# One core of a two-layer hybrid decoder trunk: side work in more steps, new wait numbers, a branch hint

## The chip, the core and the metric

The kernel runs on one core of a Trainium2 chip. A core has five engines, each with an instruction queue of its own that is worked off in order: TensorE (PE: matmuls, with weight loads shown apart as PEld), VectorE (DVE), ScalarE (ACT), GpSimd (POOL) and SyncE (SP), which here only issues DMA transfers. An engine waits for another through semaphores, and an instruction that waits holds all that stand behind it on its queue. The metric is the device time of one execution in microseconds (us).

## The reference

Two layers over 256 tokens of width 1024, all in float32:

```python
for i in range(2):
    h = rmsnorm(x, norm_mix[i])
    z, xbc, dt, nsa_q, nsa_kv, nsa_g, rwkv_u, swa_q, swa_kv, gates = split_cols(h @ w_in[i])
    y = [ssd(z, xbc, dt), nsa(nsa_q, nsa_kv, nsa_g), rwkv7(rwkv_u), swa(swa_q, swa_kv, positions)]
    merged = sum(sigmoid(gates[m]) * (y[m] @ w_br[m]) for m in range(4))
    x = x + merged @ w_out[i]
    h = rmsnorm(x, norm_ffn[i])
    x = x + (swiglu(h) if i % 2 == 0 else moe_top2_of_8(h))
    x = x + sigmoid(x @ ple_gate[i]) * (p[i] @ ple_proj[i])
return rmsnorm(x, norm_final)
```

The four mixers are a chunked state-space scan (ssd), sparse attention (nsa), a recurrent state update (rwkv7) and sliding-window attention (swa). Only swa uses `positions`: its queries and keys are rotated by `cos` and `sin` of position times 32 inverse frequencies.

## The kernel before

**The main stream.** The program is one list of units, worked through by `run_units` (L195). A unit is a weight panel: SP loads it as `raw` (128 x 1024 float32 at most, four buffers, L269); ACT casts it to a rounded half `H` (`L318`); DVE (`L321`) and POOL (`L323`) together make the residual `L = raw - H`, DVE three quarters of the columns and POOL one. `H` and `L` have three buffers. PE then multiplies with three products, `H` times high, `L` times high, `H` times low (`mm3`, L362 to L364). Units named `tokm` give tokens by 416 or 512 columns, units named `fm` give features by 256 tokens. The activations' own halves are made in the same way by `split_to`: a cast on ACT (`L371`) and a subtraction on DVE (`L372`). In a trace a tile's name tells what it is: `qTH` and `qTL` the halves of a query, `krH` and `krL` those of the rotated key, `yeH` that of an expert's output.

**The side work.** The mixers' own work, all that is not a product with a weight panel, is written as Python generators in a list `side`: `rwkv_half` (twice a layer), `ssd`, `nsa`, `swa`, and in layer 0 also `rope_tables` (the rotary tables, L516 to L542) and `cast` (constants to bf16, L172). The main stream calls `tick()` at fixed points between its matmuls. A tick takes 0.64 off every generator's counter, and a generator whose counter is used up emits its next step, up to its next `yield`. How many ticks it then rests stands in the table `WAITS`, by the generator's name with the count of its use and by the number of the step; where the table has no entry, the yielded number divided by 0.64 and rounded up holds (1.2 where nothing is yielded). So the table sets where in each engine's queue a step's instructions stand between the instructions of the main stream; nothing is moved at run time. All of it is in one in-order queue per engine: a side step that waits on POOL or ACT holds the next panel's `L` or `H` there.

**The names in the steps.** In `rwkv_half`: `v`, `k`, `r` are shifted mixes (L672 on ACT, L673 on DVE), `kkn` (L770), `kp` (L774 DVE, L775 POOL), `AR` (L780 DVE, L781 POOL), `beta` (L783, L785), `bq` (L792), then the matmuls `bop` (L797) and `gram` (L823); `kap` (L787) is POOL's. `LO` and `XT` (L838, L846) belong to the inversion of a triangular matrix, with the matmuls `m`, `dx`, `dxt` (L812). In attention, `nm` (L1141, DVE) is a row maximum and `Pm` (L1145, ACT) the exponential that follows it; `rraw` (L1368) is a query or key copied out for the rotation, which takes a matmul (L1385), two operations on DVE (L1387, L1389: `rtmp`) and one on POOL (L1388), and then `split_to`. In `ssd`, `wT` is a decay (L1071 on ACT, L1072 on DVE).

**The end.** Layer 1 ends with eight experts. `overflow` (L1994 to L1998) is a branch on a value read on the chip: where an expert has more than 128 tokens, a second pass of all experts runs; with these inputs it doesn't, and each engine jumps over that pass. What follows is the sum of the last expert's output (`yeH`, `sct`) and the last per-layer product.

Of the kernel before, what the change touches and what calls it, by code (L numbers as in the profile page):

```python
# [19 lines left out]
P = 128  # L20
# [28 lines left out]
def _consts():  # L49
# [37 lines left out]
    for k, v in cols.items():  # L87
# [10 lines left out]


WAITS = {  # L100
# [19 lines left out]
}  # L120


def trunk_kernel(tc, I, out, dbg=None, upto=99):
# [38 lines left out]
    def late_consts(place):  # L162
        stages = []
        for c in range(NC32, NCST, 512):
            w = min(512, NCST - c)
            stages.append((c - NC32, w, place("stage")))
            nc.sync.dma_start(stages[-1][2][:, :w], I["consts"][:, c:c + w])

        def cast():
            yield 8.0  # L170
            for c, w, t in stages:
                nc.gpsimd.tensor_copy(cstb[:, c:c + w], t[:, :w])  # L172
        return cast

    def K(name):
        o, w = COFF[name]
        return cst[:, o:o + w] if o < NC32 else cstb[:, o - NC32:o - NC32 + w]
# [16 lines left out]
    def psb(name="psb"):  # L194
        return psB.tile([P, 512], F32, tag="b", name=name)  # L195
# [24 lines left out]
    def wait_of(g, d):  # L220
        return WAITS.get(g[2], {}).get(g[3], math.ceil(d / 0.64 - 1e-3)) * 0.64

# [25 lines left out]
    def until(*names):  # L248
        while not all(n in flags for n in names):
            yield "poll"  # L250
# [118 lines left out]
    def split_to(H, L, src, scale=None):  # L369
        if scale is None:  # L370
            nc.scalar.copy(H, src)  # L371
            tt(L, src, H, ALU.subtract)  # L372
        else:
            act(H, src, AF.Copy, scale=scale)  # L374
            stt(L, src, scale, H, ALU.mult, ALU.subtract)  # L375
# [19 lines left out]
    def dma2(dst, src):  # L395
        nc.sync.dma_start(dst, src)
# [121 lines left out]
    def rope_tables(place):  # L518

        pool = nc.gpsimd  # L520
        pos, scr = place("pos"), place("scr")
        posi = pos.bitcast(I32)[:, 0:S]
        ang, nn = scr[:, 0:S], scr[:, S:2 * S]
        dma2(posi, I["positions"].to_broadcast([P, S]))
        pool.tensor_copy(ang, posi)
        pool.tensor_scalar(ang, ang, K("invf"), None, ALU.mult)
        magic = 12582912.0
        pool.tensor_scalar(nn, ang, 1.0 / (2 * math.pi), magic, ALU.mult, ALU.add)
        pool.tensor_scalar(nn, nn, magic, None, ALU.subtract)
        c1 = 6.28125  # L530
        c2 = 0.0019350051879882812
        c3 = 2 * math.pi - c1 - c2
        for c in (c1, c2, c3):
            pool.tensor_scalar(cosT, nn, -c, None, ALU.mult)
            pool.tensor_tensor(ang, ang, cosT, ALU.add)
        yield 12.0
        ts(ang, ang, math.pi, -math.pi, ALU.min, ALU.max)
        stt(nn, ang, -1.0, ang, ALU.mult, ALU.max)
        ts(nn, nn, -1.0, math.pi / 2, ALU.mult, ALU.add)
        yield 2.0  # L540
        act(sinT, ang, AF.Sin)
        act(cosT, nn, AF.Sin)  # L542
# [9 lines left out]
    def mixing(l, after):  # L552
        Z = SimpleNamespace(y={}, mxa=None)
# [98 lines left out]
        def branch_out(name, pool, bufs=2):  # L652
            H = pool.tile([P, 4, S], F32R, tag="yH", name="yH" + name, bufs=bufs)
            L = pool.tile([P, 4, S], F32R, tag="yL", name="yL" + name, bufs=bufs)
            Z.y[name] = (H, L)
# [529 lines left out]
        def key_tile(tag, bufs=1):  # L1185

            kz = tuple(Z.mxa.tile([P, 2, S], F32R, tag=tag + c, name=tag + c, bufs=bufs) for c in "HL")
            for t in kz:
                for g in range(2):
                    nc.gpsimd.memset(t[HD[1 - g], g].bitcast(F32), 0.0)  # L1190
            return kz

        def query_tile():
            return tuple(Z.mxa.tile([P, 4, S], F32R, tag="qT" + c, name="qT" + c, bufs=2) for c in "HL")

        def pv(o, voff, PT, first, last):
            for g in range(2):
                sl = HD[g]
                v0 = Z.vtok[:, 0, voff + g * 64:voff + g * 64 + 64]
                v1 = Z.vtok[:, 1, voff + g * 64:voff + g * 64 + 64]  # L1200
                mm(o[sl, 0:S], v0, PT[:, g, 0:S], start=first, stop=False)
                mm(o[sl, P:S], v1, PT[:, g, S:384], start=False, stop=last)
# [173 lines left out]
        def swa():  # L1376
            mxa = Z.mxa
            qs = query_tile()
            ks = key_tile("kr")
            for n in range(5):  # L1380
                yield from until(F(f"rr{n}."))
                yield 2.0
                raw = rr[n]
                rp = psb("rotp")[:, :S]
                mm(rp, K("rot"), raw, start=True, stop=True)  # L1385
                t = mxa.tile([P, S], F32, tag="rt", name="rtmp", bufs=2)
                tt(t, rp, sinT, ALU.mult)  # L1387
                nc.gpsimd.tensor_tensor(raw, raw, cosT, ALU.mult)  # L1388
                tt(t, t, raw, ALU.add)  # L1389
                if n:  # L1390
                    split_to(qs[0][:, n - 1], qs[1][:, n - 1], t)
                else:
                    for g in range(2):
                        split_to(ks[0][HD[g], g], ks[1][HD[g], g], t[HD[g]])
            nsk = mxa.tile([P, 4, 2], F32, tag="nsk", name="nsk")
            ts(nsk, Z.snk.rearrange("p (g r) -> p r g", g=2), -1.0, None, ALU.mult)
            branch_out("swa", Z.mxa, 1)
            def use(PT, r):
                o = psb("so")[:, :S]
                pv(o, 256, PT, True, True)  # L1400
                head_out("swa", r, o)

            yield from until(F("nsa"))
            yield from attn_pipe([(qs, ks, r, None, True, nsk[:, r], lambda PT, r=r: use(PT, r)) for r in range(4)])
            flags.add(F("swa"))
# [40 lines left out]
        if l == 0:  # L1446
            unit(None, spawn=[lambda: rope_tables(R)])
# [287 lines left out]
    def moe(l, Z):  # L1735
# [252 lines left out]

        def load_most():
            Z.most = nc.values_load(Z.mxi[0:1, 0:1], min_val=0, max_val=S)  # L1990
            tc.mark_branch_hint_location("overflow")

        experts(0)

        def overflow():
            with tc.If(Z.most > P, label="overflow"):
                keep = list(stream)
                stream.clear()  # L1998
                experts(P)
                mine = list(stream)  # L2000
                stream[:] = keep
                with tc.tile_pool(name="ovr", bufs=2) as r2, tc.tile_pool(name="ovs", bufs=2) as s2:
                    run_units(mine, Slots(r2, 2, s2, 2))
            if f"xffn{l}" in dbg:
                for i in range(2):
                    nc.sync.dma_start(dbg[f"xffn{l}"][i], x[:, i])
# [5 lines left out]
    for l in range(DEPTH):  # L2012
        if upto <= 10 * l:
            break
        Z = SimpleNamespace(ctx=ExitStack(), GT={}, OHT={}, rc={}, before=None, after=None)
# [35 lines left out]
```

## Time and profile before

| | before |
|---|---|
| median of 3 runs | 2006.41 us (2005.33 to 2008.68) |
| the profiled execution | 2005.13 us |
| its span in the trace | 2003.3 us |
| PE busy | 1938.6 us (97%) |
| DVE, ACT, POOL busy | 77%, 59%, 56% |
| mean granted clock of TensorE | 0.989 |

The span falls into mixing of layer 0 (0 to 475 us), its dense feed-forward block with the per-layer product (475 to 700), mixing of layer 1 (700 to 1160), the experts (1160 to 1950) and the end (1950 to 2003). A timeline row is one or several like instructions in a row: start, busy time, engine, line, operation, output and inputs; in square brackets the idle time of the engine just ahead of it and what ended it. [...]

### The profile page before, as it was taken

What the parts mean: (1) busy time and instruction counts of PE and PEld (TensorE: products, weight loads), DVE (VectorE), ACT (ScalarE), POOL (GpSimd) and SP (SyncE); (2) the same over time, 40 slices, a digit from 0 to 9 for tenths busy, and PEclk for the clock granted to TensorE, in tenths of its full rate; (3) what the DMA queues carried; (4) which work ended last, traced back from release to release, by engine and by line L of the source; (5) the groups of instructions that cost most, each with busy time, mean ns of one, the idle gap of its engine ahead of it and who ended that gap; (6) DMA issues with size and microseconds to landing.
All of it is one profiled execution on the core that took longest, in us unless ns stands there. A gap on an engine that the chain in (4) does not pass through costs nothing. (4 is left out here: it accounts for less than half of the span.)

```text
span 2003.3 us, 37459 instructions
## 1 busy us (share of the span) xinstructions
PE 1938.6 (97%) x13236; PEld 1606.8 (80%) x13236; DVE 1533.7 (77%) x2432; ACT 1176.9 (59%) x1786; POOL 1120.4 (56%) x976
## 2 busy tenths in 40 slices
PE   7999999999999899999999999999999999999997
PEld 6798897778999788878777777778777877787775
DVE  6475756766555666656666589999999999999996
ACT  5333445545444443334455567777877787778773
POOL 4543254454555254414354666777767767777773
PEclk9999999999999999999999999999999999999998
DMA  7322464457665453228354889999999999999973
GB/s 202 96 75 82 111 146 137 117 160 216 187 189 166 115 133 93 76 85 163 102 146 137 280 270 354 313 330 351 360 354 331 347 362 357 328 349 362 354 255 107
DMA packets 419441, 435.78 MB, mean 218 GB/s; under 512 B 67876, under 2 KB 355624, under 8 KB 419240
## 3 DMA queue, kind: packets, MB, share of 16 engines
q1 hardware_dynamic: 419240, 433.26, 69.1%
q8 instruction: 106, 1.74, 0.4%
q14 instruction: 95, 0.78, 0.1%
HBM read 432.13 MB, written 1.05 MB: 216 GB/s over the span
## 5 line engine op out<-in xcount | busy, mean ns | idle before, releaser
L323 POOL TENSOR_TENSOR L<-raw,H 128x256 fp32r<-128x256 f32 (+1 forms) x794 | 950.8, 1207 | 808.7 <-ACT H L318 608.8
L321 DVE TENSOR_TENSOR L<-raw,H 128x768 fp32r<-128x768 f32 (+1 forms) x792 | 933.3, 1207 | 169.2 <-ACT H L318 166.7
L318 ACT CAST H<-raw 128x1024 fp32r<-128x1024 f32 x794 | 828.6, 1047 | 227.0 <-issue 44.8
L362 PE MATMUL gu<-H,GH 128*128 128x512 f32 x704 | 286.5, 407 | 0.1
L363 PE MATMUL gu<-L,GH 128*128 128x512 f32 x704 | 279.3, 397 | 0.5 <-DVE L L321 0.5
L364 PE MATMUL gu<-H,GL 128*128 128x512 f32 x704 | 278.1, 395 | 1.1 <-DVE GL L375 1.1
L364 PE MATMUL dn<-H,aL 128*128 128x512 f32 x440 | 173.9, 395 | 1.6 <-DVE aL L372 1.6
L363 PE MATMUL dn<-L,aH 128*128 128x512 f32 x440 | 174.5, 397 | 0.0
L362 PE MATMUL dn<-H,aH 128*128 128x512 f32 x440 | 174.3, 396 | 0.2 <-ACT pj L1576 0.2
L362 PE MATMUL fm<-hTH,H 128*128 128x256 f32 x560 | 166.9, 298 | 0.0
L363 PEld LDWEIGHTS gu<-L,GH 128*128 128x128 f32 x704 | 132.5, 188 | 41.1 <-DVE L L321 15.0
L363 PE MATMUL fm<-hTL,H 128*128 128x256 f32 x560 | 157.8, 282 | 0.0
L364 PE MATMUL fm<-hTH,L 128*128 128x256 f32 x560 | 157.5, 281 | 0.0
L364 PEld LDWEIGHTS gu<-H,GL 128*128 128x128 f32 x704 | 132.4, 188 | 29.0 <-DVE GL L375 2.7
L362 PEld LDWEIGHTS gu<-H,GH 128*128 128x128 f32 x704 | 132.3, 188 | 27.3 <-ACT GH L374 0.6
L362 PE MATMUL tokm<-H,hTH 128*128 128x512 f32 (+1 forms) x320 | 139.1, 435 | 4.4 <-ACT H L318 4.4
L363 PE MATMUL tokm<-L,hTH 128*128 128x512 f32 (+1 forms) x320 | 126.8, 396 | 5.6 <-POOL L L323 4.0
L364 PE MATMUL tokm<-H,hTL 128*128 128x512 f32 (+1 forms) x320 | 126.4, 395 | 0.0
L362 PEld LDWEIGHTS fm<-hTH,H 128*128 128x128 f32 x560 | 106.4, 190 | 5.9 <-issue 2.7
L363 PEld LDWEIGHTS fm<-hTL,H 128*128 128x128 f32 x560 | 106.4, 190 | 0.2
L364 PEld LDWEIGHTS fm<-hTH,L 128*128 128x128 f32 x560 | 106.2, 190 | 0.0
L363 PEld LDWEIGHTS dn<-L,aH 128*128 128x128 f32 x440 | 82.6, 188 | 23.8 <-DVE L L321 7.6
(507 smaller groups left out, 3520.2 us busy)
## 6 DMA issues: line engine op xcount, KB each, us to landing
raw<-moe_w_gate SPq DMA_DIRECT2D x341, 256.0 KB
raw<-moe_w_up SPq DMA_DIRECT2D x341, 256.0 KB
raw<-moe_w_down SPq DMA_DIRECT2D x169, 512.0 KB
raw<-w_in SPq DMA_DIRECT2D x126, 512.0 KB
raw<-ffn_w_gate SPq DMA_DIRECT2D x22, 512.0 KB
raw<-ffn_w_up SPq DMA_DIRECT2D x22, 512.0 KB
raw<-ffn_w_down SPq DMA_DIRECT2D x22, 512.0 KB
raw<-w_in SPq DMA_DIRECT2D x32, 256.0 KB
```

The source lines that it names most:

```text
L318: nc.scalar.copy(H[:, :n], raw[:, :n])
L321: tt(L[:, :m], raw[:, :m], H[:, :m], ALU.subtract)
L323: nc.gpsimd.tensor_tensor(L[:, m:n], raw[:, m:n], H[:, m:n], ALU.subtract)
L362: mm(o, l[0], r[0], start=start, stop=False)
L363: mm(o, l[0], r[1], start=False, stop=False)
L364: mm(o, l[1], r[0], start=False, stop=stop)
```

## The change

The whole table `WAITS` is written anew. Two generators that had no entries get some, `cast0` and `rope_tables0`, and `swa` has five steps more, so that its entries are counted differently. In the code four places change: `cast` ends a step after each of its three casts; `rope_tables` ends a step after the positions' transfer is issued, after each two of its operations on POOL and after each pair of the last six (before, all ten stood in one step); `swa` ends a step ahead of each rotary split; and the branch gets a hint instruction for all engines that it is likely taken, and is written the other way round (`Z.most <= P` with an empty body and the experts in `Else`, marked as not preferred to fall through). No operation on data is added or removed.

```diff
 WAITS = {
+    'cast0': {0: 18, 1: 1, 2: 5, 3: 6, 4: 1},
...
+    'rope_tables0': {0: 2, 2: 1, 3: 8, 4: 8, 5: 9, 6: 1, 7: 9},
...
             for c, w, t in stages:
                 nc.gpsimd.tensor_copy(cstb[:, c:c + w], t[:, :w])
+                yield
...
         dma2(posi, I["positions"].to_broadcast([P, S]))
+        yield 2.5
         pool.tensor_copy(ang, posi)
         pool.tensor_scalar(ang, ang, K("invf"), None, ALU.mult)
+        yield 1.2
         magic = 12582912.0
         pool.tensor_scalar(nn, ang, 1.0 / (2 * math.pi), magic, ALU.mult, ALU.add)
         pool.tensor_scalar(nn, nn, magic, None, ALU.subtract)
+        yield 1.2
...
         for c in (c1, c2, c3):
             pool.tensor_scalar(cosT, nn, -c, None, ALU.mult)
             pool.tensor_tensor(ang, ang, cosT, ALU.add)
-        yield 12.0
+            yield 1.2
...
                 tt(t, t, raw, ALU.add)
+                yield 1.2
                 if n:
                     split_to(qs[0][:, n - 1], qs[1][:, n - 1], t)
...
             Z.most = nc.values_load(Z.mxi[0:1, 0:1], min_val=0, max_val=S)
-            tc.mark_branch_hint_location("overflow")
+            tc.mark_branch_hint_location("overflow", "LikelyTaken", engines=list(mybir.ALL_ENGINES))
...
-            with tc.If(Z.most > P, label="overflow"):
+            with tc.If(Z.most <= P, label="overflow", preferred_fallthrough_block=False) as fits:
+                pass
+            with fits.Else():
                 keep = list(stream)
```

Where instructions move: the line numbers of the changed program are 6 to 10 higher. On POOL in layer 0, at the values panels (the `L` of 192 columns), before:

```order
15 L775 TENSOR_TENSOR kp<-kp,k 128x512
16 L781 TENSOR_TENSOR AR<-r,Dd 128x8x64
17 L525 CAST scr<-pos 128x256
18 L526 TENSOR_SCALAR scr<-scr,cst 128x256
19 L528 TENSOR_SCALAR scr<-scr 128x256
20 L529 TENSOR_SCALAR scr<-scr 128x256
21 L534 TENSOR_SCALAR cosT<-scr 128x256
22 L535 TENSOR_TENSOR scr<-scr,cosT 128x256
...
27 L323 TENSOR_TENSOR L<-raw,H 128x192
28 L787 TENSOR_TENSOR kap<-kp,inv 128x512
29 L323 TENSOR_TENSOR L<-raw,H 128x192
30 L323 TENSOR_TENSOR L<-raw,H 128x256 x2
```

and now:

```order
16 L784 TENSOR_TENSOR kp<-kp,k 128x512
17 L177 CAST cstb<-stage 128x192
18 L329 TENSOR_TENSOR L<-raw,H 128x192
19 L790 TENSOR_TENSOR AR<-r,Dd 128x8x64
20 L796 TENSOR_TENSOR kap<-kp,inv 128x512
21 L329 TENSOR_TENSOR L<-raw,H 128x192
22 L532 CAST scr<-pos 128x256
23 L533 TENSOR_SCALAR scr<-scr,cst 128x256
24 L536 TENSOR_SCALAR scr<-scr 128x256
25 L537 TENSOR_SCALAR scr<-scr 128x256
26 L329 TENSOR_TENSOR L<-raw,H 128x256 x2
27 L543 TENSOR_SCALAR cosT<-scr 128x256
```

Behind the first of its pairs the rows of before leave out two like pairs. The third and the fourth `L` of 192 columns now stand ahead of the rotary operations, and these are no longer in one piece. SP's issue of the positions moves behind one more panel of `w_in`:

```order
43 L269 DMA raw<-w_in 128x8x128 x2
44 L396 DMA pos<-positions 128x256
45 L269 DMA raw<-w_in 128x8x128 x12
46 L269 DMA raw<-w_in 128x2x512 x12
47 L269 DMA raw<-w_br_ssd 128x2x512 x4
```

is before, and now it is:

```order
44 L275 DMA raw<-w_in 128x8x128 x3
45 L402 DMA pos<-positions 128x256
46 L275 DMA raw<-w_in 128x8x128 x11
47 L275 DMA raw<-w_in 128x2x512 x12
48 L275 DMA raw<-w_br_ssd 128x2x512 x4
```

Three of the `fm` panels are loaded ahead of the positions, and not two. On ACT in layer 0, at the rotary split of the first queries, before:

```order
165 L1145 ACTIVATE Pm,ls<-sc,nm 128x128 x2
166 L1368 ACTIVATE rraw<-fm 128x256
167 L318 CAST H<-raw 128x1024
168 L371 CAST qTH<-rtmp 128x256
169 L1145 ACTIVATE Pm,ls<-sc,nm 128x256 x2
170 L1368 ACTIVATE rraw<-fm 128x256
171 L371 CAST qTH<-rtmp 128x256
172 L318 CAST H<-raw 128x1024
173 L1368 ACTIVATE rraw<-fm 128x256
```

and now:

```order
165 L1154 ACTIVATE Pm,ls<-sc,nm 128x128 x2
166 L377 CAST krH<-rtmp 64x256 x2
167 L1377 ACTIVATE rraw<-fm 128x256
168 L324 CAST H<-raw 128x1024
169 L1154 ACTIVATE Pm,ls<-sc,nm 128x256 x2
170 L1377 ACTIVATE rraw<-fm 128x256
171 L324 CAST H<-raw 128x1024
172 L377 CAST qTH<-rtmp 128x256
173 L1377 ACTIVATE rraw<-fm 128x256
```

The second cast `H` of these rows stood behind two casts `qTH` and stands behind none. The hint comes at the start of every queue; on ACT it is:

```order
0 L2059 UNCONDITIONAL_BRANCH
1 L2059 BRANCH_PREFETCH_HINT
2 L437 ACT_TABLE_LOAD
3 L437 ACTIVATE junk,ssq<-x 128x512 x4
4 L324 CAST H<-raw 128x1024
```

where before the queue went from the first branch straight to the table load; the instructions around the later branch itself stand as they did.

## Rows read from the trace of the kernel before

**Rows 1.** The page, part 1: busy us (share of the span) and instructions.

```profile
PE 1938.6 (97%) x13236; PEld 1606.8 (80%) x13236; DVE 1533.7 (77%) x2432; ACT 1176.9 (59%) x1786; POOL 1120.4 (56%) x976
```

**Rows 2.** Windows: us, busy PE, PEld, DVE, ACT, POOL, then PEclk, DMA share, GB/s.

```profile
0.00:475.00 475.00, 448.34 (x4029) 379.40 (x4030) 302.46 (x652) 215.56 (x430) 209.98 (x190) 0.99 0.49 132
...
1160.00:1950.00 790.00, 785.90 (x3518) 620.91 (x3518) 775.76 (x892) 625.45 (x756) 574.86 (x523) 1.00 0.99 337
```

**Rows 3.** PE's timeline at place A, 44 to 62 us.

```profile
48.53 0.46 PE L363 MATMUL tokm<-L,hTH 128*128 128x416 f32 x1 [0.43 <-DVE L L321]
...
50.99 1.37 PE L797 MATMUL bop<-bq,cst 128*128 128x512 f32 x2 [1.82 <-DVE bq L792]
...
58.55 0.72 PE L363 MATMUL tokm<-L,hTH 128*128 128x416 f32 x1 [3.64 <-POOL L L323]
```

**Rows 4.** POOL's timeline, 30 to 60 us.

```profile
34.70 1.47 POOL L172 CAST cstb<-stage 128x512 bf16<-128x512 f32 x3
...
45.55 1.64 POOL L781 TENSOR_TENSOR AR<-r,Dd 128x512 f32<-128x512 f32 x1
48.13 0.60 POOL L525 CAST scr<-pos 128x256 f32<-128x256 int32 x1 [0.94 <-DMA pos<-positions]
...
51.29 1.43 POOL L529 TENSOR_SCALAR scr<-scr 128x256 f32<-128x256 f32 x1
...
57.91 0.59 POOL L323 TENSOR_TENSOR L<-raw,H 128x192 fp32r<-128x192 f32 x1
```

**Rows 5.** DVE's timeline, 40 to 62 us.

```profile
42.69 0.87 DVE L770 SCALAR_TENSOR_TENSOR kkn<-k,par,spr 128x256 f32<-128x256 f32 x2
...
44.12 0.48 DVE L673 SCALAR_TENSOR_TENSOR v<-fm,par,v 128x255 f32<-128x255 f32 x1
44.52 1.62 DVE L780 SCALAR_TENSOR_TENSOR AR<-kkn,Dd 128x512 f32<-128x512 f32 x1
...
49.93 1.01 DVE L792 SCALAR_TENSOR_TENSOR bq<-r,par,kp 128x256 f32<-128x256 f32 x2
```

**Rows 6.** Windows of PE alone: us, PE busy, PEclk, DMA share, GB/s.

```profile
52.00:54.00 2.00, 2.00 (x17) 0.50 0.00 0
...
58.00:60.00 2.00, 1.45 (x4) 0.64 0.15 17
60.00:62.00 2.00, 2.00 (x16) 0.50 1.06 279
302.00:308.00 6.00, 5.69 (x15) 0.52 0.50 138
988.00:990.00 2.00, 2.00 (x7) 0.50 0.60 224
1964.00:1970.00 6.00, 5.19 (x15) 0.50 0.49 178
```

**Rows 7.** PE's timeline at place B, 294 to 312 us.

```profile
302.11 0.80 PE L362 MATMUL tokm<-H,hTH 128*128 128x512 f32 x1 [3.33 <-ACT H L318]
```

**Rows 8.** ACT's timeline at place B, 290 to 312 us.

```profile
300.71 0.40 ACT L371 CAST qTH<-rtmp 128x256 fp32r<-128x256 f32 x1 [1.67 <-DVE rtmp L1389]
301.02 1.04 ACT L318 CAST H<-raw 128x1024 fp32r<-128x1024 f32 x1
```

**Rows 9.** PE's timeline at place B1, 983 to 987 us.

```profile
984.79 0.49 PE L362 MATMUL tokm<-H,hTH 128*128 128x512 f32 x1 [1.04 <-ACT H L318]
```

**Rows 10.** The branch's line L1996 by queue: duration ns, first and last start us.

```profile
L1996 PEldq COMPARE_BRANCH  x1: 5230/5230/5230, 1956.4 to 1956.4; - x1
```

**Rows 11.** ACT's timeline behind the branch, 1955 to 1966 us.

```profile
1961.79 0.58 ACT L371 CAST yeH<-dn 128x512 fp32r<-128x512 f32 x1 [5.09 <-PEq L1996]
```

**Rows 12.** PE's timeline behind the branch, 1961 to 1966 us.

```profile
1962.43 0.49 PE L1918 MATMUL sct<-yeH,OHT 128*128 128x512 f32 x1 [3.50 <-ACT yeH L371]
```

**Rows 13.** SP's queue, 40 to 90 us: start, us, the issues.

```profile
43.20 0.57 SPq L396 DMA_DIRECT2D pos<-positions  x1
58.52 27.41 SPq L269 DMA_DIRECT2D raw<-w_in  x7
```

**Rows 14.** DVE's waits, 30 to 475 us: total us, times, longest us.

```profile
DVE wT L1072 <- ACT wT L1071: 8.8, 4, 3.0
```

35 rows, old and new, of the table WAITS are left out of this document.

## Prediction

> **What bounds the kernel now.** I read the busy shares first: TensorE (PE) is at work for 1938.6 of 2003.3 us, the others for 77% or less [rows 1]. So only what stops or slows PE counts. By stages it stops least in the experts (1160 to 1950 us, busy 785.9 of 790) and far more in the first mixing stage (448.34 of 475), where most of the change lies [rows 2]. [...] I price a place as idle time plus busy time x (1 - clock). Four places matter.
>
> Place A, 46 to 63 us. PE idles 0.43, 1.82 and 3.64 us, together 5.89, before three matmuls [rows 3]. The longest wait ends on POOL: the 192-column share of the third values panel's residual L (L323) runs at 57.91, right behind ten operations of the rotary tables that hold POOL from 48.13 on [rows 4]. Its other parts were ready: DVE's last L for it ended as bq began, at 49.93 [rows 5]. The three slowed slices lose 2.00 x 0.50 + 1.45 x 0.36 + 2.00 x 0.50 = 2.5 us [rows 6]. Place A costs 8.4 us.
>
> Place B, 298 to 308 us. PE idles 3.33 us for a cast H (L318) [rows 7]. On ACT that cast starts at 301.02, just behind the rotary cast qTH, which itself stood 1.67 us for DVE's rotary sum [rows 8]. From 302 to 308 the clock is 0.52 over 5.69 busy us: 2.7 lost [rows 6]. Place B costs 6.1 us.
>
> Place B1 is the same in layer 1: 1.04 us idle [rows 9] and one slice at half clock, 1.0 us [rows 6]: 2.0 us.
>
> The branch, 1956 to 1962 us: PE's compare-and-branch takes 5.23 us [rows 10], the cast of yeH on ACT stands 5.09 us after it [rows 11], and the first scatter matmul 3.50 us for that cast [rows 12].
>
> **The change, part by part.** The profiled execution took 2005.13 us, 1.28 less than the median of 2006.41; I sum against the former and add 1.3 at the end.
>
> *Rotary tables and late casts in steps (A).* POOL's order becomes kp, a short cast, third L192, AR, kap, fourth L192, then four of the rotary operations; the three pairs that remain come later, one at a time. AR ended at 47.2 [rows 4], so the third L192, now ahead of it, is there long before PE asks at about 55, and the 3.64 us go. The 0.43 go too: DVE's L now stands ahead of AR, which took it 1.62 us [rows 5]. Each wide cast takes about 0.5 us (the three took 1.47, [rows 4]) and now stands ahead of one of the first two L192; PE did not wait for those, so I take nothing.
>
> What is late next is bq: kkn, which began at 42.69, is queued behind the second v step, at 44.12 [rows 5], so bq slips by 1.4 to 1.7 us. The bop matmul that wants it comes one triple of tokm matmuls (0.6 us) later, so its wait of 1.82 becomes 2.7. Waits: -3.64 - 0.43 + 0.9 = -3.2. Of the 2.5 us lost to the clock half should go with the second gap: -1.3. **A: -4.5**, between -2.0 (bop worse, clock as it was) and -7.0.
>
> *The positions' transfer.* SP issued it at 43.20, and the next weight panel only at 58.52 [rows 13], as the third L192, at 57.91, gave its raw buffer back. Now that panel stands ahead of the positions on SP. With the third L192 done at about 49 the panel goes then and the positions a moment after, about 50; at the 4.9 us that they took before (43.20 to 48.13), they land at 55. POOL, whose fourth L192 is done by 52, stands 3 us for them, and then the four operations (48.13 to 52.72, [rows 4]) take 4.6 us: the next 256-column share of L starts at about 59.6. PE asks for it after the fourth panel, some 11 us of matmuls after the gap that goes, at about 66. I cost it at nothing; were that cover gone, it would be up to 7.6 us of POOL standing in the way.
>
> *The wait ahead of the rotary split (B).* Each yield sends other queued work ahead of qTH and qTL. In ACT's new order the late H stands ahead of qTH, behind two exponentials (Pm) and a copy (rraw); on DVE the maximum nm that these exponentials need is no longer behind the rotary sums and qTL. If nm comes as soon as it can, H is cast by about 297.4, and PE, which asks at 298.8, does not stop: -6.1. If the exponentials and rraw run where they ran, until 299.04 (300.71 - 1.67), H follows at once and is there at 300.1, not at 302.06 [rows 8]: 2.0 us less gap and about the same clock loss, -2.0. I take **-5.5**, near the first end, since all that nm has lost from its queue is work that waited. *B1* is the same edit with less at stake: **-2.0**, between 0 and -3.
>
> *The hint.* [...] Of the 3.50 us that PE idled, 0.9 is the cast's own way (0.58 and the signals to and fro), so 2.6 us go. If the shorter gap keeps the clock up, some of the 5.19 x 0.50 = 2.6 us lost from 1964 to 1970 comes back [rows 6]; how much is unknown, so I count a quarter, 0.7. **-3.3**, from 0 (no effect) to -5. The hint is one instruction more on each queue: nothing.
>
> *All other waits* reorder the state updates, the decays and the sparse attention, beside a PE that is over 94% busy there. Their sign is open: **0**, from -3 to +5.
>
> Sum: -4.5 - 5.5 - 2.0 - 3.3 = -15.3, so 2005.1 - 15.3 = 1989.8, and 1991.1 against the median.
>
> **The rivals.**
>
> *The hint does nothing.* It is the second instruction of each queue, and the branch comes at 1956 us [rows 10], some nine thousand rows down PE's list. [...] Then 3.3 us are missing: 1994.4. [...]
>
> *The stops only change places.* At A bop becomes the long wait, at B the exponentials set H (-2.0 each), B1 gives nothing, the hint half (-1.6), and new small stops cost 2: -3.6, so 2002.8. For it: at A and at B a second wait stands within a few us of the first [rows 3, 8], and one of them is always next.
>
> *Slower.* The decay steps of ssd (wT, L1071 and L1072) are retimed, and DVE stands at them with the small copies behind it that feed the recurrence's matmuls in PE's main order. In the first layer DVE waits 8.8 us at four such steps, up to 3.0 each [rows 14], so far without cost to PE. One us of idle PE costs about 1.6 here (A 8.4 / 5.89, B 6.1 / 3.33). To lose the 15.3 and 4 more, 12 us of waiting must reach PE: two thirds of 17.6, if layer 1 holds as much. With 14 us: 22.4 - 15.3 = +7, 2013. Against it: the panels' L are made ahead of need, and most of these steps keep their neighbours.
>
> *More goes than I count.* The far ends of all terms: -7.0 - 6.1 - 3 - 5 - 3 = -24.1: 1982.3.
>
> **How the numbers follow.** My forecast 0.45, no effect of the hint 0.25, places changed 0.14, slower 0.07, more 0.09. The time is the likeliest case's, 1991. The range runs from the last rival's 1982 to 2002, just short of the changed places; outside lie most of that case, the slower one and a little below: 2 in 10. A measurement of this kernel tells about 0.2%, 4 us, from no change. Faster by more (below 2002.4) are the forecast, the first and last rivals and a fifth of the changed places: 0.82. Within: most of the rest of that case, 0.11. Slower: 0.07.
>
> **What would show it.** In the changed profile: PE's wait for POOL's L near 55 us gone, a bop wait of 2 to 3 us still there, POOL's cast of the positions standing for their transfer; no wait for H near 300 and a clock of 1.00 from 302 to 308; PE's compare-and-branch well below 5 us, or still 5.2 if the hint is idle. PE's idle time in the first stage should fall from 26.7 us to about 20. I am wrong if qTH, set back, makes a score matmul wait instead, if the first panels after the values wait for POOL near 66 us, or if DVE's wT waits show up as idle time of PE between 180 and 215 us.

## The result and the profile after

The changed kernel takes 1982.08 us (median of 4, 1980.57 to 1984.18) where the kernel before took 2005.87 beside it: a ratio of 0.9883, with a 95% interval of 0.9870 to 0.9895, 23.8 us. The forecast was 1991, 14.9 us, in a range from 1982 to 2002: the direction is right, and the time lies at the range's lower edge. The profiled execution took 1981.97 us, with a span of 1980.2.

The page's first part for the changed kernel, busy us and shares, against [rows 1]:

```profile
PE 1924.7 (97%) x13236; PEld 1598.9 (81%) x13236; DVE 1532.5 (77%) x2432; ACT 1177.8 (59%) x1786; POOL 1119.7 (57%) x976
```

PE is still the bound, and it is busy 14 us less with the same 13236 matmuls: more than half of the gain is not idle time but matmuls that take less time. Most of that is TensorE's clock: its mean granted clock rose from 0.989 to 0.994, and busy time x (1 - clock), summed over the run, fell from 16.1 to 7.0 us. Where the gain arises is read from PE's own order. Both programs have the same main-stream matmuls in the same sequence, so that the start of a certain one in either trace tells how far the changed kernel leads. The first panel behind the ssd output product, as PE's timelines have it, before and after:

```profile
246.84 0.28 PE L362 MATMUL fm<-hTH,H 128*128 128x256 f32 x1
```

```profile
239.92 0.28 PE L368 MATMUL fm<-hTH,H 128*128 128x256 f32 x1
```

That is a lead of 6.9 us. Up to each of these places both programs have run the same number of PE instructions. The same reading at five more places, for the changed kernel and for the runs that undo or isolate a part (us, against the profile of before; the columns are PE's first matmul of the stage named, and the last `tokm`):

| run | behind ssd | dense block | mixing 1 | experts | branch | end |
|---|---|---|---|---|---|---|
| before, at | 246.84 | 477.97 | 699.66 | 1160.18 | 1958.53 | 1993.13 |
| changed kernel | 6.9 | 14.5 | 12.5 | 19.5 | 19.3 | 23.1 |
| hint alone | -0.6 | -0.7 | -1.0 | 1.4 | 1.1 | 4.9 |
| rotary tables and casts alone | 3.2 | 2.8 | 3.2 | 4.5 | 4.7 | 1.5 |
| rotary split alone | -0.8 | 6.4 | 5.4 | 11.5 | 11.1 | 7.3 |
| other waits alone | 0.7 | 0.2 | 0.4 | 2.9 | 2.4 | 1.5 |
| all but the other waits (the four mixers' old rows) | 1.6 | 9.2 | 8.9 | 15.4 | 14.9 | 18.7 |

So the changed kernel wins 6.9 us before 247 us, 7.6 up to the dense block, loses 2.0 around it, wins 7.0 in mixing 1 and 3.8 at the branch. The experts give nothing and lose nothing. A row is one profiled execution: the runs with the hint alone and with the turned condition alone, which leave everything ahead of the branch in the order of before, differ from the profile of before by up to 1.5 us there.

**Place A.** PE's timeline of the changed kernel, 46 to 64 us, against [rows 3]:

```profile
49.86 0.46 PE L369 MATMUL tokm<-L,hTH 128*128 128x416 f32 x1 [1.75 <-POOL L L329]
...
51.45 1.13 PE L806 MATMUL bop<-bq,cst 128*128 128x512 f32 x2 [0.95 <-DVE bq L801]
```

Idle time is down from 5.89 to 2.70 us. POOL's timeline there, against [rows 4], and SP's issue of the positions, against [rows 13]:

```profile
44.91 3.02 POOL L784 TENSOR_TENSOR kp<-kp,k 128x512 f32<-128x512 f32 x1 [3.22 <-DVE kp L783]
47.88 0.80 POOL L177 CAST cstb<-stage 128x192 bf16<-128x192 f32 x1
48.65 1.16 POOL L329 TENSOR_TENSOR L<-raw,H 128x192 fp32r<-128x192 f32 x1
...
54.16 0.40 POOL L532 CAST scr<-pos 128x256 f32<-128x256 int32 x1 [0.37 <-DMA pos<-positions]
```

```profile
50.24 0.58 SPq L402 DMA_DIRECT2D pos<-positions  x1
```

The rotary operations stand behind the fourth panel's L, and the positions land in time for them. But `kp` takes 3.02 us, where it took 1.29. On DVE `bq` begins at 49.28, a little earlier than the 49.93 of [rows 5], and takes 2.12 us where it took 1.01:

```profile
49.28 2.12 DVE L801 SCALAR_TENSOR_TENSOR bq<-r,par,kp 128x256 f32<-128x256 f32 x2
```

**Place B.** ACT's timeline of the changed kernel, 280 to 300 us, against [rows 8], and PE's clock from 290 on, against [rows 6] (PEclk, the number behind PE's busy time, is the granted clock as a share of the full one):

```profile
287.70 1.06 ACT L324 CAST H<-raw 128x1024 fp32r<-128x1024 f32 x1
289.94 0.41 ACT L377 CAST qTH<-rtmp 128x256 fp32r<-128x256 f32 x1 [1.18 <-DVE rtmp L1398]
```

```profile
290.00:300.00 10.00, 10.00 (x50) 1.00 0.55 163
```

The cast H is made 2.2 us before the rotary cast that it used to stand behind, and PE neither waits nor slows.

**The branch.** Line L2006 by queue in the changed kernel, against [rows 10], then ACT and PE behind it, against [rows 11, 12]:

```profile
L2006 PEldq COMPARE_BRANCH  x1: 423/423/423, 1937.0 to 1937.0; - x1
```

```profile
1939.75 0.59 ACT L377 CAST yeH<-dn 128x512 fp32r<-128x512 f32 x1 [2.69 <-PEq L2006]
```

```profile
1940.39 0.50 PE L1928 MATMUL sct<-yeH,OHT 128*128 128x512 f32 x1 [0.81 <-ACT yeH L377]
```

The branch takes 0.42 us where it took 5.23. The cast starts 0.2 us after PE's last `dn` matmul has ended, and the gap ahead of the first scatter matmul is 0.81 us where it was 3.50. A part of that comes back as a longer wait for DVE's `x`, before and after:

```profile
1969.44 0.47 PE L386 MATMUL trp<-cst,x 128*128 128x128 f32 x1 [0.35 <-DVE x L1926]
```

```profile
1946.33 0.33 PE L392 MATMUL trp<-cst,x 128*128 128x128 f32 x1 [1.28 <-DVE x L1936]
```

### The profile page after: what moved, and what is told of

Its sections match the earlier page's. It is cut to its first block, busy times and chain, and to the rows that moved or that the text cites. A ratio compares the mean times of both kernels' runs of the same rounds, so it can differ in the third digit from the quotient of the medians.

```text
span 1980.2 us, 37485 instructions
## 1 busy us (share of the span) xinstructions
PE 1924.7 (97%) x13236; PEld 1598.9 (81%) x13236; DVE 1532.5 (77%) x2432; ACT 1177.8 (59%) x1786; POOL 1119.7 (57%) x976
## 5 line engine op out<-in xcount | busy, mean ns | idle before, releaser
L369 PEld LDWEIGHTS dn<-L,aH 128*128 128x128 f32 x440 | 82.6, 188 | 23.8 <-DVE L L327 7.6
```

The source lines that it names most:

```text
L369: mm(o, l[0], r[1], start=False, stop=False)
```

## The experiments

Each is the kernel before or the changed kernel with one part put in or taken out. Times are medians beside runs of the kernel before on the same chip.

**The hint, three ways.** The hint with the turned condition:

```diff
-            tc.mark_branch_hint_location("overflow")
+            tc.mark_branch_hint_location("overflow", "LikelyTaken", engines=list(mybir.ALL_ENGINES))
...
-            with tc.If(Z.most > P, label="overflow"):
+            with tc.If(Z.most <= P, label="overflow", preferred_fallthrough_block=False) as fits:
+                pass
+            with fits.Else():
```

> The kernel before with only the branch changed, hint and turned-round condition together. If the branch part stands by itself: PE's compare-and-branch falls from 5.23 us to about 0.4, the gap ahead of the first scatter matmul from 3.50 to about 0.8, no slow clock behind it, and 3.5 to 4 us off (about 2002). If the short branch of the changed kernel hung on its other edits: 5.2 us again and no change (2006).

the first pair of lines alone:

> The kernel before with the hint instruction alone, the condition as it was. If the hint is what shortens the branch: as with both, 0.4 us in PE's branch and 3.5 to 4 us off. If the hint needs the turned condition: 5.2 us and no change.

the second alone:

> The kernel before with the turned condition alone, no hint. If the hint does it: PE's branch 5.2 us, no change (2006). If the other layout of the branch does it: 0.4 us and 3.5 to 4 us off.

With both, 2001.07 us against 2006.2 (0.9978, 0.9969 to 0.9988); the hint alone, 2000.77 (0.9977, 0.9967 to 0.9986); the turned condition alone, 2006.49 (1.0000, 0.9990 to 1.0009). The branch's line in the run with the hint alone, and in the one with the turned condition alone:

```profile
L1996 PEldq COMPARE_BRANCH  x1: 423/423/423, 1955.3 to 1955.3; - x1
```

```profile
L1996 PEldq COMPARE_BRANCH  x1: 5166/5166/5166, 1954.9 to 1954.9; - x1
```

It is the hint, in all of the 4.5 us, and the turned condition shows no effect. PE is not the only engine that the jump holds. On ACT and DVE the compare itself took 0.05 and 0.07 us in the kernel before and 0.07 and 0.09 with the hint alone, but their next instruction came 4.5 and 4.7 us after it in the kernel before, and 1.1 and 1.0 us after it with the hint alone. With the turned condition alone it is DVE that the cast of yeH stands for last:

```profile
1961.05 0.59 ACT L371 CAST yeH<-dn 128x512 fp32r<-128x512 f32 x1 [5.87 <-DVEq L1996]
```

One thing that was expected did not come: with both edits a stretch at half clock still followed the branch and cost 1.5 us. Over all profiled runs here, half clock behind the branch cost 2.8 to 5.8 us in the seven without a hint and 0 to 1.7 us in the seven with one. In the changed kernel the hint runs at 0.8 us on PE, some 1936 us ahead of the branch, and the branch takes 0.42 us all the same: the rival that the hint does nothing did not come.

**The rotary tables and the late casts alone.**

```diff
+    'cast0': {0: 18, 1: 1, 2: 5, 3: 6, 4: 1},
+    'rope_tables0': {0: 2, 2: 1, 3: 8, 4: 8, 5: 9, 6: 1, 7: 9},
...
                 nc.gpsimd.tensor_copy(cstb[:, c:c + w], t[:, :w])
+                yield
```

and the six new `yield`s of `rope_tables`, in place of the one that stood there.

> The kernel before with the rotary tables and the late casts in steps, with the two new rows of the table for them, everything else as before. If the ten rotary operations on POOL are what the third values panel waited for: PE's 3.64 us for POOL's L are gone, the bop wait of 1.8 us stays, and 4 to 6 us go (about 2001). If the mixing waits around it set the gain: the wait goes from POOL to another engine and less than 2 us go.

2003.17 us, 0.9987 (0.9978 to 0.9997): 2.6 us, between the two cases expected (4 to 6, under 2). The two gaps that PE's timeline shows at this place (44 to 66 us):

```profile
48.59 0.46 PE L359 MATMUL tokm<-L,hTH 128*128 128x416 f32 x1 [0.67 <-DVE L L317]
52.52 1.92 PE L796 MATMUL bop<-bq,cst 128*128 128x512 f32 x2 [3.28 <-DVE bq L791]
```

The 3.64 us for POOL's L are gone, the bop wait has grown from 1.82 to 3.28 and the first gap from 0.43 to 0.67: nearly half of the 3.64 only changed places. Nothing in DVE's order differs there. What differs is how long DVE takes, here in this run (40 to 56 us), and then in the kernel before (47 to 51 us):

```profile
46.72 1.82 DVE L317 TENSOR_TENSOR L<-raw,H 128x640 fp32r<-128x640 f32 x1
...
49.46 1.88 DVE L317 TENSOR_TENSOR L<-raw,H 128x640 fp32r<-128x640 f32 x1
51.26 1.20 DVE L791 SCALAR_TENSOR_TENSOR bq<-r,par,kp 128x256 f32<-128x256 f32 x2
```

```profile
47.66 0.81 DVE L321 TENSOR_TENSOR L<-raw,H 128x640 fp32r<-128x640 f32 x1
...
49.20 0.81 DVE L321 TENSOR_TENSOR L<-raw,H 128x640 fp32r<-128x640 f32 x1
```

The same subtraction takes 0.81 us beside POOL's rotary operations and 1.82 to 1.88 beside POOL's AR, L and kap, which now stand in their stead. bq begins 1.3 us later for it.

**Whether two inputs on POOL do that.**

```diff
-        pool.tensor_scalar(ang, ang, K("invf"), None, ALU.mult)
+        pool.tensor_tensor(ang, ang, ang, ALU.add)
...
-            pool.tensor_scalar(cosT, nn, -c, None, ALU.mult)
+            pool.tensor_tensor(cosT, nn, nn, ALU.add)
```

and the two operations between them likewise.

> The kernel before with the seven rotary operations on POOL that read one tensor (multiply or add a constant) written as additions of a tensor to itself, which read two; same place, same sizes; the rotary tables hold other values. If operations with two tensor inputs on POOL and on DVE keep each other out: DVE's L of 640 columns and beta and bq between 47.7 and 51 us take 1.2 to 1.9 us where they took 0.8 to 1.0, bq ends 1 to 2 us later, and the bop wait grows from 1.8 to about 3. If POOL's two-input operations don't matter to DVE: DVE's rows keep their durations.

DVE's timeline (44 to 58 us) and PE's gaps (44 to 60 us) in this run:

```profile
49.32 1.23 DVE L321 TENSOR_TENSOR L<-raw,H 128x640 fp32r<-128x640 f32 x1
50.47 1.58 DVE L792 SCALAR_TENSOR_TENSOR bq<-r,par,kp 128x256 f32<-128x256 f32 x2
```

```profile
52.10 1.12 PE L797 MATMUL bop<-bq,cst 128*128 128x512 f32 x2 [2.82 <-DVE bq L792]
...
57.50 0.72 PE L363 MATMUL tokm<-L,hTH 128*128 128x416 f32 x1 [1.86 <-POOL L L323]
```

As expected: beside the two-input forms the L takes 1.23 us for 0.81, bq 1.58 for 1.01, and the bop wait is 2.82 us for 1.82. The L at 47.78 kept its 0.81; POOL was waiting or at its cast then. beta, from 48.51, kept its 0.88 although POOL's first two-input operation ran beside its second half, from 48.93; that operation itself took 0.94 us, where like ones later took 0.61 to 0.67. The block on POOL itself ended 1.0 us sooner, so PE's wait for L fell as well, and the time (2003.46, 0.9990, 0.9980 to 1.0000) says nothing by itself.

**One piece, later.**

```diff
+    'rope_tables0': {0: 12},
```

> The kernel before with one number: the rotary tables start 12 ticks later, still in one piece of ten operations. If only their place ahead of the third panel's L counts: the 3.64 us go and 4 to 6 us are gained, as with the steps. If the piece has to be cut: the ten operations, 9.8 us on POOL, now hold the residual of a later panel or the LO steps, PE stops there for 2 us or more, and little is gained.

2004.30 us, 0.9992 (0.9982 to 1.0001). In the trace the lead behind ssd is 3.0 us, against 3.2 with the steps: place does nearly all of it. The rival that the piece has to be cut did not come: no new wait for a later L or for LO appeared. The bop wait is 3.43 us here, 1.6 more than before, and the 4 to 6 us did not come either.

**The rotary split alone.**

```diff
                 tt(t, t, raw, ALU.add)
+                yield 1.2
                 if n:
```

and the new rows `swa0` and `swa1`.

> The kernel before with the step ahead of the rotary split and the two new rows of the table for the sliding-window mixer, everything else as before. If this edit carries both layers: about 6.5 us off by 312 us, and about as much again by the end of mixing 1, 12 to 13 in all (about 1993). If layer 1 gains by the other mixers' waits: 6 to 8 us off (about 1999), the place at 984 us mended and no more.

1996.26 us, 0.9946 (0.9929 to 0.9963): 9.1 us off the 2005.4 beside it by the medians, 10.8 by the ratio, whose interval (7.4 to 14.2 us) holds both. That lies between the two cases expected. It is the largest part: 7.2 us between 247 and 478 us, and 6.1 in mixing 1. PE's clock at place B in this run, against [rows 6]:

```profile
302.00:308.00 6.00, 6.00 (x31) 1.00 0.71 192
```

In mixing 1 PE waited before for more than the cast at 984.79, and of the waits shown here only the one for Pm is left. PE's waits there, 930 to 1126 us, first in the kernel before, then in this run (total us, times, longest us):

```profile
PE tokm L362 <- ACT H L318: 1.0, 1, 1.0
PE tokm L363 <- DVE L L321: 1.0, 2, 0.5
PE sc L362 <- ACT Pm L1145: 0.8, 1, 0.8
...
PE sc L362 <- DVE rtmp L1387: 0.4, 1, 0.4
```

```profile
PE sc L355 <- ACT Pm L1138: 1.0, 1, 1.0
```

**The other mixers' waits, taken out and alone.** The changed kernel with the old rows for `rwkv_half`, `ssd`, `nsa` and `keep`, and the kernel before with the new ones:

```diff
-    'rwkv_half0': {1: 6, 3: 3, 4: 3, 5: 2, 6: 5, 8: 1, 10: 4, 12: 1, 15: 3, 16: 4, 17: 4, 18: 2, 20: 5, 21: 2,
+    'rwkv_half0': {1: 5, 3: 3, 4: 3, 6: 5, 8: 1, 10: 4, 12: 1, 15: 3, 16: 4, 17: 4, 18: 2, 20: 5, 21: 2, 22: 4,
...
```

> The changed kernel with the old rows of the table for rwkv_half, ssd, nsa and keep; rotary tables, casts, rotary split and hint as changed. If the other mixers' new waits are worth nothing, as in the forecast: the same 1982. If they carry part of the gain: 1984 to 1988, with more idle time of PE between 60 and 240 us or in mixing 1.

> The kernel before with only the new rows for rwkv_half, ssd, nsa and keep. Counterpart of the run before: no change (2006) if they are worth nothing, 2 to 6 us off if they carry part of the gain by themselves; slower if they only fit the other edits, with a third values panel that waits longer for POOL, since its second triple now stands ahead of the bop matmul.

Taken out: 1987.27 us, 0.9908 (0.9892 to 0.9925), by the ratios 5 us more than the changed kernel, though the two intervals just touch. Alone: 2004.09, 0.9994 (0.9984 to 1.0003), nothing that can be told. So these waits are worth something together with the rotary steps, and no gain shows without them. PE's gaps at place A show why; without them in the changed kernel, and then alone:

```profile
53.01 2.08 PE L796 MATMUL bop<-bq,cst 128*128 128x512 f32 x2 [3.28 <-DVE bq L791]
```

```profile
58.25 0.72 PE L356 MATMUL tokm<-L,hTH 128*128 128x416 f32 x1 [9.94 <-POOL L L316]
```

The new rows put one triple of tokm matmuls ahead of bop. With the rotary operations still in one piece on POOL, that triple wants POOL's L before they end, and PE stands 9.94 us; with the steps, it fills a part of the bop wait, 3.28 to 0.95, at the price of its own 1.75. From 42 to 72 us PE idles 2.7 us in the changed kernel and 4.0 without these waits, and loses 1.7 and 2.9 us to the clock: about half of the 5.3 us that lie between the two at 247 us. Of the rest, 0.8 stood before place A, and 2 are not assigned. The sum of the three parts by their ratios is 4.6 (hint) + 2.6 (tables) + 10.8 (split) = 18.0, and the run with all three has 18.4; the changed kernel has 23.5. Each of these has an interval of two to three and a half us either way.

**What is left at A, and at 108 us.** Two numbers of the changed kernel's table:

```diff
-    'cast0': {0: 18, 1: 1, 2: 5, 3: 6, 4: 1},
+    'cast0': {0: 18, 1: 1, 2: 5, 3: 14, 4: 1},
```

> The changed kernel with one number: the third late cast on POOL 8 ticks later, behind the fourth panel's L and no longer just ahead of the third's. If POOL's queue sets the third panel's wait (1.75 us on POOL's L at 49.9): the cast's 0.8 us come off that wait, 0.8 to 1.3 us in all. If the bop matmul behind it takes over (0.95 us there now): its wait grows by what the first lost, and the time stays.

```diff
-    'rope_tables0': {0: 2, 2: 1, 3: 8, 4: 8, 5: 9, 6: 1, 7: 9},
+    'rope_tables0': {0: 2, 2: 1, 3: 4, 4: 4, 5: 4, 6: 1, 7: 5},
```

> The changed kernel with the rotary tables' steps sooner, so that the two Sin activations on ACT stand ahead of the decay exponentials (Dd), as in the kernel before, and not ahead of the first convolution's tanh. If the table load of 1.28 us ahead of that tanh makes DVE and then the m matmul late: PE's 1.2 us for X near 108 us are gone, 1 to 1.5 us off. If that wait has another cause: it stays. If the rotary pairs, now closer together between the LO steps, hold them: a new wait of m for POOL's LO.

> The changed kernel with both of these. If the two waits are independent: the sum, about 1980; if not: no better than the better one.

The later cast: 1984.10 us (0.9892, 0.9874 to 0.9910). PE's waits between 42 and 240 us in the changed kernel, and with the later cast:

```profile
PE tokm L369 <- POOL L L329: 1.8, 1, 1.8
PE m L821 <- DVE X L866: 1.2, 1, 1.2
PE bop L806 <- DVE bq L801: 0.9, 1, 0.9
```

```profile
PE bop L796 <- DVE bq L791: 2.8, 1, 2.8
PE m L811 <- DVE X L856: 1.2, 1, 1.2
PE tokm L359 <- POOL L L319: 0.9, 1, 0.9
```

The wait for L fell by 0.9 us and the bop wait grew by 1.9, more than the other lost. On POOL, AR and then kap (from 51.12 on) now run beside nearly the whole of DVE's bq; first POOL's timeline, then DVE's in this run (40 to 60 us):

```profile
49.40 1.75 POOL L780 TENSOR_TENSOR AR<-r,Dd 128x512 f32<-128x512 f32 x1
```

```profile
50.05 2.79 DVE L791 SCALAR_TENSOR_TENSOR bq<-r,par,kp 128x256 f32<-128x256 f32 x2
```

bq took 2.12 us in the changed kernel and 1.01 in the kernel before. The earlier Sin: 1983.31 us (0.9882, 0.9861 to 0.9902). The wait of m for X is gone. In the changed kernel ACT loads a table ahead of the first Sin, at 96.85 us, and another one ahead of the tanh, at 105.70, 1.28 us each; with Sin ahead of Dd the wait behind the second one is gone, so that I take it to have been this load. PE waits 1.4 us elsewhere instead, in the timeline's words `ssp` for ACT's `sq`, which stands behind Dd. In the kernel before, where Sin also stands ahead of Dd and the load at 83.98 between them, that wait was 0.4 us. With both: 1985.38 us (0.9892, 0.9873 to 0.9911). None of the three can be told from the changed kernel's 0.9883.

## Why the forecast came out as it did

**The sum.** 14.9 us were forecast and 23.8 came. By terms, forecast and measured: A 4.5 and 6.9 up to 247 us, other waits included; B 5.5 and 7.6; B1 2.0 and 7.0; the hint 3.3 and 3.8 in the trace, 4.5 in the times; minus 2.0 around the dense block, which were not forecast. The slow clock was priced at busy time x (1 - clock), and the rows of the kernel before bear that out: `tokm` matmuls of 512 columns begin 0.43 us apart from 305.43 us on, where the clock is 0.50, and 0.23 to 0.24 us apart from 322.00 on, where it is 1.00. All other waits, forecast at 0, have no stretch of their own: their 4 to 5 us lie for the most part in the 6.9. The direction and the main places were forecast; the gain was 9 us larger, and the range held the time by 0.1 us.

**A: the sum of the waits right, by errors that cancel.** The step that failed reads "is there long before PE asks at about 55". A little later the prediction has bop one triple of tokm matmuls later, and it did not apply this to the L that the triple needs: PE asks at 48.1, not 55. And POOL did not have the L by then, since `kp` took 3.02 us and not 1.29. So 1.75 us of the 3.64 stayed; but bop waited 0.95 and not 2.7, because that triple's own wait lies in front of it. The slip of bq by 1.4 to 1.7 us did not come either: it began 0.65 us earlier and took 1.11 us longer. Together the waits are 2.70, what I had as 0 + 2.7, and that is luck. Of the 6.9 us, 3.2 are these waits and 1.6 the clock (0.94 over 42 to 72 us, 0.89 before; I had 1.3). 0.5 stood before place A, and the small waits behind it cancel. Some 1.6 us are left, matmuls that take less time where the clock shows as full, and I can't assign them.

**The positions' transfer: right.** SP issued it at 50.24 (forecast 50), POOL's cast began at 54.16 (55), and the share of L behind the four operations at 57.0 (59.6), with PE asking for it at 63.2. POOL stood 0.37 us for them, and not 3. It cost nothing.

**B: right, and all of it.** The cast H moved ahead of qTH, PE asked and did not wait, and the clock stayed at 1.00: the first of the two ends weighed, 6.1 us. No score matmul waited for the later qTH. What I missed is small: a wait of 0.9 us at 403 us (`so` for `PT`) went with the same edit.

**B1: mis-sized.** I looked at the one cast at 984.79. The same edit took away 2.7 us of waits in mixing 1 (1.0, 1.0, 0.4, and 0.3 that the run with the hint alone shows), where I had counted 1.04. Of the 7.0 us, 2.4 are not the change's: the runs with the hint alone and with the turned condition alone have the order of before in mixing 1 and yet lead the profile of before by 2.4 and 2.5 us there. The kernel before at 984 us, [rows 6 and 9], lost 1.0 us and more to the slow clock. Seven profiled runs have the same two gaps there, 1.04 and 0.50 us; the slow clock followed in two of them, the kernel before and the one with hint and turned condition. The run with the hint alone has none:

```profile
985.02 0.49 PE L362 MATMUL tokm<-H,hTH 128*128 128x512 f32 x1 [1.04 <-ACT H L318]
986.02 0.50 PE L363 MATMUL tokm<-L,hTH 128*128 128x512 f32 x1 [0.50 <-DVE L L321]
```

```profile
988.00:990.00 2.00, 2.00 (x11) 1.00 0.64 232
```

Against such a run the rotary split is worth some 4 us in mixing 1. Half of the 2.0 us lost around the dense block is the same chance, the other way. In the changed kernel the clock is 0.79 from 460 to 468 us, behind waits of 1.57 and 0.43 us; the kernel before has these waits at 475 us and keeps full clock:

```profile
460.00:468.00 8.00, 7.19 (x46) 0.79 0.07 19
```

```profile
475.00:483.00 8.00, 7.57 (x58) 1.00 0.04 6
```

All profiled runs have these two waits, and the slow clock followed in two of them, this one and the rotary split alone. The other half is 0.8 us of small waits and was not followed up.

**The hint: right, its rival wrong; the terms mis-sized.** I had the price by PE's gap, 2.6 us, and a quarter of the slow clock, 0.7. That the hint would take the branch's time off this gap was my estimate, and no run shows what that time consists of; the runs show its length, 0.42 to 0.43 us with the hint and over 5 without. The gap fell by 2.7, but 0.9 of it came back in the wait for `x`, and over the whole end PE idles only 1.3 us less. The clock stayed at 1.00 behind the branch in this execution, and all of its 3.0 us came back; other runs with the hint lost up to 1.7 again. In the runs without a hint the branch took between 5.0 and 6.3 us; the profile of before, with 5.23, has one of the shorter ones.

**The other waits: the step that failed most.** "Their sign is open: 0" was right for these waits alone (0.9994) and wrong by 4 to 5 us for them beside the rotary steps. I had treated two parts as a sum that work on the same PE gap: one clears POOL for the third panel, the other uses that to fill the bop wait.

**The rivals.** The time, 1982.08, is that of "more goes than I count" (1982.3, chance 0.09), but not by its terms: A came at its far end, B and above all B1 (7.0 for 3) beyond theirs, the hint short of it (3.8 for 5), and 2.0 went the other way. "The stops only change places" came in part, for the rotary tables alone (nearly half of the 3.64) and for the later cast. The slower case did not come: PE's idle time between 160 and 240 us is zero in the changed kernel. PE's idle time in the first stage fell from 26.7 to 19.7 us (to 460.5), as said.

## What to carry to other kernels

Where two edits move work at the same gap, price them together: ask for each what it does to the wait that the other leaves. When an operation is moved on GpSimd, look which VectorE operations it then runs beside, and price both at their longer rows, not at those of the old place. A gap on TensorE had two prices here, with and without the slower clock after it: behind 1.04 and 0.50 us near 985 us the mean clock from 982 to 992 us was 0.83 in the kernel before and 1.00 with the hint alone. One profile shows one of them, so look at several before you price it.

## What the runs showed of the hardware

- The branch over the experts' second pass took 5.0 to 6.3 us on PE in the programs without a hint, and 0.42 to 0.43 us in those with one, where the hint ran at the start of each queue (0.7 to 0.8 us in the changed kernel) and the branch came at 1937 us and later. On ACT and DVE the time to the next instruction fell from 4.5 and 4.7 us to 1.1 and 1.0 (kernel before, hint alone).
- VectorE and GpSimd operations that read two tensors took longer side by side: 0.81 to 1.88 us for a subtraction of 640 columns (kernel before, rotary tables alone), 1.01 to 2.79 for bq (kernel before, later cast), 1.29 to 3.02 for kp on POOL (kernel before, changed kernel). With nothing but POOL's rotary operations turned from one tensor to two, that subtraction went from 0.81 to 1.23 us and bq from 1.01 to 1.58. Either side was at times the one that paid: beside kp's 3.02 us, DVE's AR and first beta took 0.68 us each, where they took 1.62 and 1.68 in the kernel before.
- The same two gaps on PE, 1.04 and 0.50 us, were followed by half clock in two of seven profiled runs and by full clock in five; 1.57 and 0.43 us by half clock in two of fourteen.
- A table load on ACT took 1.28 us, at 80.64 and 83.98 us in the kernel before and at 96.85 and 105.70 in the changed one. Behind the load at 105.70 PE waited 1.2 us for X; with Sin ahead of Dd it waited 1.4 us for `sq`, and 0.4 us in the kernel before.
